# Running the first latent product chunk by chunk, and turning a rarely taken block into loops

## The chip, the cores and the metric

The kernel runs on one core of one Trainium2 chip. The metric is the device time of one execution, in microseconds. Three runs of the kernel before gave 951.0, 952.68 and 953.88 us; their median is 952.68 us. The profile below is of one further execution.

## The reference

The program is a trunk of two layers over 256 tokens of width 1024, batch 1, all in float32. Each layer adds two branches to the residual stream:

```python
mod = silu(c) @ ada_w[l] + ada_b[l]          # shift, scale and gate for both branches
h = rmsnorm(x, norm1_g[l]) * (1 + sc1) + sh1
x = x + g1 * token_mix(h, positions, w_in[l], ...)
h = rmsnorm(x, norm2_g[l]) * (1 + sc2) + sh2
x = x + g2 * grouped_moe(h, w_router, ...)
```

`token_mix` projects `h` once into several sections. One of them is the latent section (384 columns for the queries, 256 for keys and values, 32 for a rotary key) of a multi-head latent attention; the others feed a gated linear recurrence (HGRN2) and the gates. The rotary parts use cos and sin of `positions * inv`. `grouped_moe` picks 2 of 16 experts for each token; every expert has a gate, an up and a down matrix.

## The kernel before

Activations lie transposed, model dimension on the 128 partitions: `xT` is eight blocks (index k) of 128x256. Weights are loaded in float32, in pieces of up to 2 MB, into buffers named A0, A1, B0, B1, C0, C1, x0, x1 and some smaller ones. A weight of the mixer is split into a rounded float32r part and the rest (`split`: a copy on ACT, a subtraction on DVE, L417), so is the activation (`hh`, `hl`), and a product is three matmuls (high x high, low x high, high x low). The split weights live in a ring of four slots (`W`, filled by `wunit`).

The framework traces the program and then orders each engine's instructions by a plan of its own: what is ready goes first, earlier program text before later. Instructions passed to `keep_in_program_order`, the loads through `load` among them, stay behind what was traced before them on their engine. SP issues all DMAs, in one queue.

Layer 0 starts as follows. Before any product, the shift and scale columns of the first norm must be made from `ada_w`: eight quarter matrices of 1 MB, `first[i, q]` with i = 1 for scale and i = 0 for shift and q the quarter of the model dimension. Each quarter is summed over the contraction by eight float32 calls on PE (`ada_rows`, L360), copied out by ACT (`part`, L368), and folded into columns by two small products and a DVE addition (`ada_finish`, L372 to L375). `modulate` (L521 to L528) then makes two blocks of `hh` and `hl` from a normalised block `h` and the columns. The loop at L609 runs the latent product in two halves of the contraction, k = 0..3 with weights `lat` half 0 and k = 4..7 with half 1; within a half the loop over the six output tiles is outside and the four blocks k inside. `first_mod` (L470) runs quarters 0 and 1 before the product begins, and quarters 2 and 3 one sum at a time between the output tiles of the first half. The weights are queued in the order: `vec`, `crow` (the vector c on all partitions), `xT`, positions, four quarters, `lat` half 0 whole, four quarters, `lat` half 1.

`tables` (L425) makes cos and sin of the rotary angles and the lower bounds of the recurrence on DVE and ACT. It stands ahead of the first norm in the program. `masks` follows the latent product. After the latent product come the sections `qf` (four pairs of output tiles), the latents' norms, and the rest of the mixer; while it runs, DVE also works off `ada_steps`, one-megabyte pieces of `ada_w` for the later columns (L384), which use `crow`.

In the mixture of experts each expert has 64 places. `overflow` (L1168) holds a block for tokens beyond them. It is under `tc.If(over > CAP)`, near the end of each layer's mixture, and each engine loads a count and branches over the block (L1172) when no expert is overfull. Inside it lies one loop over expert pairs p, whose body is written out for both experts q and the eight blocks `fb` of the hidden width (`spill`).

Of the kernel before, what the change touches and what calls it, by code (L numbers as in the profile page):

```python
# [19 lines left out]
P = 128  # L20
# [81 lines left out]
def _lay_out(v):  # L102
# [35 lines left out]
    for i, n in enumerate(("w_gate", "w_up", "w_down")):  # L138
# [3 lines left out]
        if i == 2:  # L142
# [5 lines left out]
         "adat": adat, "crow": v["c"], "we": we}  # L148
# [8 lines left out]
def trunk(ctx: ExitStack, tc: tile.TileContext, x, pos, vec_in, msk_in, lat_in, wb, wq_in, wkv_in, ada_in, adat_in, crow_in, we,  # L157
# [47 lines left out]
    nc.sync.dma_start(vec, vec_in)  # L205
# [5 lines left out]
    crow = one.tile([P, D], F32, name="crow")  # L211
    nc.sync.dma_start(crow, bass.AP(tensor=crow_in.tensor, offset=crow_in.offset, ap=[[0, P], [1, D]]))
    xT = one.tile([P, J, T], F32, name="xT")
    nc.sync.dma_start(xT, x)
    posi = solo("vm", [P, T], I32)
    nc.sync.dma_start(posi, bass.AP(tensor=pos.tensor, offset=pos.offset, ap=[[0, P], [1, T]]))
# [5 lines left out]

    def first_load(h):
        for q in (h, h + 1):
            for i in (1, 0):
                nc.sync.dma_start(first[i, h][:, (q - h) * QUART:(q - h + 1) * QUART], ada_in[i, q])

    first_load(0)
# [3 lines left out]
    for l in range(DEPTH):  # L232
        todo.append([("sec", l, n, h) for n in ("lat",) + SECTIONS for h in range(2)])
        todo.append([("moe", l, p, i, h) for p in range(E // 2) for i in range(3) for h in range(2)
                     if (p, i, h) not in ((0, 2, 1), (1, 1, 1))])

    def issue():
        while todo and not todo[0]:
            todo.pop(0)
        for n, part in enumerate(todo[:2]):  # L240
            while part:
# [13 lines left out]
                if key[0] == "sec":  # L255
# [3 lines left out]
                    if key == ("sec", 0, "lat", 0):  # L259
                        first_load(2)  # L260
# [92 lines left out]
    ac.activation(crow, crow, AF.Silu)  # L353
# [10 lines left out]

    def ada_sum(l, s, q, w, part):
        b = bank()
        ada_rows(b[:, :QD], w)
        ac.copy(part, b[:, :QD])  # L368
        return l, s, q, part, v_("four")

    def ada_finish(l, s, q, part, col):
        b = bank()  # L372
        for j in range(2):
            mm(b[:, j:j + 1], part[:, j * P:(j + 1) * P], col, True, True)
        ve.tensor_add(mod[l][:, s, 2 * q:2 * q + 2], b[:, :2], v_("adab", (l * 6 + s) * J + 2 * q, 2))  # L375
# [32 lines left out]
    def normed(b):  # L408
        r = rstd(b)
        hs = []  # L410
        for j in range(0, J, 2):
            hs.append(t2("h"))
            ve.tensor_mul(hs[-1], xT[:, j:j + 2, :], r.unsqueeze(1).to_broadcast([P, 2, T]))
        return hs

# [6 lines left out]
    cosT = one.tile([P, T], F32, name="cosT")  # L422
    sinT = one.tile([P, T], F32, name="sinT")

    def tables():  # L425
# [4 lines left out]
        for o, off, add in ((cosT, 0.25, 1.5707963267948966), (sinT, 0.0, 0.0)):  # L430
# [9 lines left out]
            ac.activation(o, o, AF.Sin)  # L440
        ve.tensor_scalar(sinT, sinT, v_("sgn"), None, op0=ALU.mult)

        lbt = t2("lbt", [P, 4, HEADS])
# [15 lines left out]
    def masks():  # L459
        trif, mskf = t2("trif", [P, P]), solo("vm", [P, len(LEVELS) + 1, P])  # L460
# [5 lines left out]
    tables()  # L466
# [3 lines left out]
    hs0 = normed(b)  # L470

    def first_mod(h, modulate):
        last = None
        for q in (h, h + 1):
            for i in (1, 0):
                part = wk.tile([P, QD], F32, tag="acc", bufs=2, name=nm("part"))
                part = ada_sum(0, i, q, first[i, h][:, (q - h) * QUART:(q - h + 1) * QUART], part)
                if last:
                    ada_finish(*last)
                last = part  # L480
                if (i, q) == (1, h + 1):
                    modulate(2 * h)
                yield
        ada_finish(*last)
        modulate(2 * h + 2)

    def mixer(l, hs, after):
# [33 lines left out]
        def modulate(j):  # L521
            js, h = slice(j, j + 2), hs[j // 2]
# [59 lines left out]
        ready = []  # L582
        if l == 0:
            for _ in first_mod(0, modulate):
                pass
# [30 lines left out]
        if l == 0:  # L616
            masks()
# [734 lines left out]
```

## Time and profile before

| what | value |
|---|---|
| median of three runs | 952.68 us |
| the profiled execution's own time | 950.02 us |
| its span, first to last instruction | 948.2 us |
| PE busy | 893.8 us (94%) |
| DVE busy | 502.1 us (53%) |
| ACT busy | 343.8 us (36%) |
| mean granted TensorE clock | 0.975 |
| read from HBM | 314.58 MB |

PE is TensorE's matmul, PEld its weight load. "Granted clock" is the share of TensorE's full speed. A matmul in float32 leaves two PE rows and two PEld rows for each call, one in float32r one of each. In a row of a timeline the first two numbers are start and duration in us, and the bracket tells how long the engine idled before it and what released it; a name ending in q is the engine's sequencer.

### The profile page before, as it was taken

Reading aid. Unit: us, or ns where it says so; the run is one execution under the profiler, and the core shown is the slowest. Engines: PE = TensorE matmul, PEld = TensorE weight load, DVE = VectorE, ACT = ScalarE, POOL = GpSimd, SP = SyncE. Lnnn points to the kernel's source line nnn. Section 1 sums busy time; section 2 is a strip of 40 time slices with the busy share of each in tenths; the row PEclk is TensorE's granted clock in tenths of the full one; section 3 lists DMA queues with packets and bytes.
Section 4 is the critical chain, followed back from the end, with each engine's and each line's share of the span. In section 5 each row is a group of like instructions: output and inputs, shape, how many; then the busy total and the mean of one; then the engine's idle time right before and its main releaser. Section 6 shows DMA issues by size and latency. Waiting matters only on the chain. (4 is left out here: it accounts for less than half of the span.)

```text
span 948.2 us, 15041 instructions
## 1 busy us (share of the span) xinstructions
PE 893.8 (94%) x6118; PEld 637.0 (67%) x6118; DVE 502.1 (53%) x962; ACT 343.8 (36%) x636; POOL 19.4 (2%) x22
## 2 busy tenths in 40 slices
PE   4899999989989999999879999999998999999985
PEld 3688899989944535353359989999994453535333
DVE  4469899899441323232256968969833132323214
ACT  4465454556341112111146647456542121111103
POOL 0000200000000000000000020000000000000002
PEclk9899999999999999999979999999999999999997
DMA  8995566787799899999977626666779989999981
GB/s 362 429 416 193 222 241 238 317 327 282 308 423 423 346 431 431 431 430 426 419 272 311 276 83 241 276 250 233 294 311 423 425 346 431 431 430 431 427 333 45
DMA packets 35586, 316.75 MB, mean 334 GB/s; under 512 B 3888, under 2 KB 4144, under 8 KB 13744
## 3 DMA queue, kind: packets, MB, share of 16 engines
q1 hardware_dynamic: 35504, 315.64, 81.5%
q8 instruction: 53, 0.87, 0.3%
q14 instruction: 29, 0.24, 0.1%
HBM read 314.58 MB, written 1.05 MB: 333 GB/s over the span
## 5 line engine op out<-in xcount | busy, mean ns | idle before, releaser
L559 PE MATMUL bank<-hA,x 128*128 128x256 f32 x1312 | 241.9, 285 | 5.8 <-ACT x L417 3.8
L559 PEld LDWEIGHTS bank<-hA,x 128*128 128x128 f32 x1312 | 204.5, 191 | 9.3 <-DVE x L417 4.2
L559 PE MATMUL bank<-hB,x 128*128 128x256 f32 x656 | 184.3, 281 | 0.0
L559 PEld LDWEIGHTS bank<-hB,x 128*128 128x128 f32 x656 | 125.6, 191 | 0.2
L1211 DVE TENSOR_TENSOR he<-bank,sg 128x512 f32<-128x512 f32 x16 | 11.1, 692 | 157.0 <-PE bank L1138 157.0
L1237 DVE SCALAR_TENSOR_TENSOR r<-bank,small,r 128x512 fp32r<-128x512 f32 (+1 forms) x36 | 24.7, 690 | 96.5 <-ACT r L1236 96.5
L1236 ACT ACTIVATE r<-bank,small 128x512 fp32r<-128x512 f32 (+1 forms) x36 | 22.8, 639 | 118.3 <-PE bank L1147 118.3
L1165 DVE SCALAR_TENSOR_TENSOR xT<-bank,mod,xT 128x256 f32<-128x256 f32 x128 | 52.6, 476 | 16.0 <-PE bank L182 16.0
L1131 DVE TENSOR_SCALAR o<-bank,acol,mod 128x256 f32<-128x256 f32 x32 | 17.4, 543 | 51.5 <-PE bank L182 45.8
L1147 PE MATMUL bank<-moe_2A,heT 128*64 128x512 f32 (+1 forms) x160 | 33.8, 579 | 11.4 <-PEq L1172 5.4
L1203 ACT ACTIVATE sg<-bank 128x512 f32<-128x512 f32 x16 | 9.6, 597 | 94.8 <-PE bank L1138 94.8
L1138 PE MATMUL bank<-moe_1C,o 128*64 128x512 f32 x192 | 43.3, 593 | 0.0
L1138 PE MATMUL bank<-moe_0B,o 128*64 128x512 f32 x192 | 42.3, 593 | 0.0
L1129 ACT ACTIVATE o<-bank,mod,acol 128x256 f32<-128x256 f32 x32 | 18.1, 564 | 59.4 <-DVE o L1131 52.7
L1224 ACT COPY heT<-bank 128x512 f32<-128x512 f32 x16 | 9.4, 588 | 82.1 <-PE bank L1222 82.1
L1138 PE MATMUL bank<-moe_1A,o 128*64 128x512 f32 x160 | 36.1, 593 | 0.0
L1147 PEld LDWEIGHTS bank<-moe_2A,heT 128*64 128x64 f32 x160 | 13.8, 163 | 27.7 <-issue 25.1
L1138 PEld LDWEIGHTS bank<-moe_0B,o 128*64 128x64 f32 x192 | 13.6, 137 | 26.5 <-issue 25.7
L1138 PEld LDWEIGHTS bank<-moe_1C,o 128*64 128x64 f32 x192 | 13.6, 137 | 26.5 <-issue 26.3
L1147 PE MATMUL bank<-moe_2x,heT 128*64 128x512 f32 (+1 forms) x160 | 29.6, 512 | 0.0
L182 PE MATMUL bank<-C 128*128 128x64 f32 (+1 forms) x240 | 29.2, 272 | 0.0
L1138 PE MATMUL bank<-moe_0x,o 128*64 128x512 f32 x128 | 28.6, 594 | 0.0
(304 smaller groups left out, 1669.3 us busy)
## 6 DMA issues: line engine op xcount, KB each, us to landing
moe_0B<-in_we SPq DMA_DIRECT2D x8, 2048.0 KB, 8.9
moe_1C<-in_we SPq DMA_DIRECT2D x8, 2048.0 KB, 14.6
moe_0x<-in_we SPq DMA_DIRECT2D x8, 2048.0 KB, 15.1
moe_1A<-in_we SPq DMA_DIRECT2D x6, 2048.0 KB, 11.6
moe_2A<-in_we SPq DMA_DIRECT2D x6, 2048.0 KB, 14.1
moe_1x<-in_we SPq DMA_DIRECT2D x6, 2048.0 KB, 18.0
moe_2x<-in_we SPq DMA_DIRECT2D x6, 2048.0 KB, 15.5
moe_2C<-in_we SPq DMA_DIRECT2D x6, 2048.0 KB, 20.1
```

What stands on the lines that cost most here:

```text
L182: return pe.matmul(o, l, r, start=start, stop=stop)
L559: pe.matmul(o, a[:, k, :], b[:, k0 + k, :], start=first and k == 0 and q == 0, stop=last and k == 3 and q == 2)
L1129: ac.activation(o, bq, AF.Identity, bias=sh2[:, j:j + 1], scale=acol[:, j:j + 1])
L1131: ve.tensor_scalar(o, bq, acol[:, j:j + 1], sh2[:, j:j + 1], op0=ALU.mult, op1=ALU.add)
L1138: pe.matmul(b[64 * q:64 * q + 64, :], x(j, q), w[:, o:o + 512], start=(j == 0), stop=(j == J - 1), tile_position=(0, 64 * q))
L1147: pe.matmul(b[64 * q:64 * q + 64].rearrange("p (c n) -> p c n", n=256)[:, c % 2:c % 2 + n], x[:, j, 64 * q:64 * q + 64], _ap(w[:, o:o + 25 ...
L1165: ve.scalar_tensor_tensor(xT[:, j, :], b[:, q * T:(q + 1) * T], g2[:, j:j + 1], xT[:, j, :], op0=ALU.mult, op1=ALU.add)
L1203: ac.activation(sg, bg.rearrange("s (j f) -> s j f", j=FJ), AF.Silu)
L1211: ve.tensor_tensor(he, bu.rearrange("s (j f) -> s j f", j=FJ), sg, ALU.mult)
L1224: ac.copy(heT, b.rearrange("p (j s) -> p j s", j=FJ))
L1236: ac.activation(yv[:, 0, d], b[:, s], AF.Copy, scale=wc)
L1237: ve.scalar_tensor_tensor(yv[:, 1, d], b[:, s], wc, yv[:, 0, d], op0=ALU.mult, op1=ALU.subtract)
```

## The change

1. Loads. `crow` is no longer loaded. `vec`, `xT`, the quarters and the latent weights of layer 0 go through `load` in the order: `vec`, `xT`, then for each chunk c = 0..3 the scale quarter, the shift quarter and the quarter of `lat` that belongs to blocks k = 2c and 2c+1; the positions come after chunk 0.
2. `crow` is made from `ca` (silu of c) by eight float32 products with the identity and two ACT copies.
3. The latent product of layer 0 runs over chunks of the contraction. A chunk splits its weights into two units of four output tiles and one unit (`both`) for tiles 4 and 5 of both blocks; the product of block 2c; in its midst the sums of chunk c+1 (two quarters at a time, one copy of 512 columns, four small products, one addition) and `modulate` for it. All six output tiles accumulate over the whole stage.
4. `modulate` also makes the normalised block h; `first_mod`, `ada_sum`, `ada_finish` and `normed` go.
5. `tables` and `masks` are called after the squares of the latents, cos and sin go through one ACT instruction, and a square root table is asked for at the start.
6. In `overflow` the experts q and the blocks of the hidden width become loops too (three nested loops); the body keeps two halves.

```diff
+    for c in range(4):
+        h, q = c // 2, c % 2
+        for i in (1, 0):
+            load(first[i, 2 * h][:, q * QUART:(q + 1) * QUART], ada_in[i, c])
+        n = slice(q * 2 * N_LAT, (q + 1) * 2 * N_LAT)
+        load(lat0[h][:, n], lat_in[0, h][:, n])
+        if c == 0:
+            load(posi, ...)
...
-    ac.activation(crow, crow, AF.Silu)
+    crow = one.tile([P, D], F32, name="crow")
+    for h in range(2):
+        b = bank()
+        for j in range(4):
+            mm(b[:, j * P:(j + 1) * P], ca[:, 4 * h + j:4 * h + j + 1].to_broadcast([P, P]), ident, True, True)
+        ac.copy(crow[:, h * 512:(h + 1) * 512], b)
...
+    def first_sum(c):
+        b = bank()
+        for i in (1, 0):
+            ada_rows(b[:, i * QD:(i + 1) * QD], first[i, c // 2 * 2][:, c % 2 * QUART:(c % 2 + 1) * QUART])
+        part = wk.tile([P, 2 * QD], F32, tag="acc", bufs=2, name=nm("part"))
+        ac.copy(part, b)
+        return part
+
+    def first_finish(c, part):
+        b = bank()
+        for i in range(4):
+            mm(b[:, i:i + 1], part[:, i * P:(i + 1) * P], v_("four"), True, True)
+        js = slice(2 * c, 2 * c + 2)
+        ve.tensor_add(mod[0][:, 0:2, js], ...)
...
         def modulate(j):
-            js, h = slice(j, j + 2), hs[j // 2]
+            js, h = slice(j, j + 2), t2("h")
+            ve.tensor_mul(h, xT[:, js, :], r0.unsqueeze(1).to_broadcast([P, 2, T]))
...
+        def tiles(n, k, i0, units):
+            for i in range(i0, i0 + 3):
+                wh, wl = (units[n][q][:, i] if i < 4 else units[2][q][:, 2 * (i - 4) + n] for q in range(2))
+                for q, (a, x) in enumerate(((wh, hh), (wl, hh), (wh, hl))):
+                    pe.matmul(bs[i][:, :T], a, x[:, k, :], start=k == q == 0, stop=k == J - 1 and q == 2)
...
         if l == 0:
-            for _ in first_mod(0, modulate):
-                pass
-            second = first_mod(2, modulate)
+            first_finish(0, first_sum(0))
+            modulate(0)
+            for c in range(4):
+                w = take("sec", l, "lat", c // 2)...
+                k = 2 * (c % 2)
+                units = [wunit(w[:, k + n, :4 * P]...) for n in range(2)]
+                units.append(both(w, k))
+                for i in (0, 3):
+                    tiles(0, 2 * c, i, units)
+                part = first_sum(c + 1) if c < 3 else None
+                tiles(1, 2 * c + 1, 0, units)
+                if part is not None:
+                    first_finish(c + 1, part)
+                    modulate(2 * c + 2)
+                tiles(1, 2 * c + 1, 3, units)
...
-        if l == 0:
-            masks()
...
+        if l == 0:
+            tables()
+            masks()
         w = section(l, "qf")
...
-                with tc.For_i(0, E // 2, 1) as p:
-                    for q in range(2):
-                        spill(l, p, q, hT, left[:, :, q::2], g2, room)
+                with tc.For_i(0, E // 2, 1) as p, tc.For_i(0, 2, 1) as q:
+                    spill(l, p, q, hT, left, g2, room)
...
-        for fb in range(F // n):
+        with tc.For_i(0, FJ, 1) as fj:
+            for half in range(2):
```

## Rows read from the trace of the kernel before

**Rows 1.** The page: PE's busy tenths and granted clock in 40 slices of the span.

```profile
PE   4899999989989999999879999999998999999985
...
PEclk9899999999999999999979999999999999999997
```

**Rows 2.** Stretches of the first 200 us: start:end, length, then busy us and instructions of PE, PEld, DVE, ACT and POOL, granted clock, DMA share, GB/s.

```profile
26.00:33.00 7.00, 6.24 (x32) 5.56 (x36) 4.36 (x8) 3.40 (x7) 0.00 (x0) 0.51 1.02 429
33.00:46.00 13.00, 11.83 (x128) 9.09 (x120) 3.47 (x11) 3.63 (x9) 0.00 (x0) 1.00 1.01 427
46.00:50.00 4.00, 3.28 (x13) 3.01 (x14) 3.63 (x7) 2.23 (x5) 0.00 (x0) 0.57 1.01 432
...
80.00:200.00 120.00, 118.40 (x928) 110.67 (x928) 108.44 (x182) 64.94 (x129) 6.97 (x4) 1.00 0.70 263
```

**Rows 3.** The same view of the products at L559 alone (PE and PEld): the latent product, then the first half of `qf`.

```profile
26.70:56.70 30.00, 22.46 (x144) 20.90 (x145) 0.84 1.01 427
56.70:67.60 10.90, 10.90 (x98) 10.88 (x97) 1.00 1.03 429
```

**Rows 4.** Timeline of the start, in order of time: first sums, their copy, the normalised blocks, first `hh`, first latent product.

```profile
15.95 1.93 PE L360 MATMUL bank<-first,ca 128*32 128x256 f32 x32
...
18.28 0.64 ACT L368 COPY part<-bank 128x256 f32<-128x256 f32 x2
18.41 1.75 DVE L405 RECIPROCAL rstd<-rstd 128x256 f32<-128x256 f32 x1 [1.43 <-ACT rstd L404]
...
26.76 0.58 PE L559 MATMUL bank<-hA,x 128*128 128x256 f32 x1 [1.89 <-ACT x L417]
```

**Rows 5.** Issue to landing, in us, of the quarters `first` (eight loads), of both latent halves, and of `ada_0r`'s first load, by the view of a tile; and the first use of `ada_0r`.

```profile
L226 SPq DMA_DIRECT2D first<-in_ada x8: 328/390/548, 2.6 to 12.5; - x8
DMA to landing us min/median/max: 9.9/17.5/20.4
L191 SPq DMA_DIRECT2D sec_lat_0A<-in_lat x1: 679/679/679, 4.8 to 4.8; - x1
DMA to landing us min/median/max: 18.2/18.2/18.2
L191 SPq DMA_DIRECT2D sec_lat_1A<-in_lat x1: 328/328/328, 14.9 to 14.9; - x1
DMA to landing us min/median/max: 21.1/21.1/21.1
L384 DVE CUSTOM_DVE_ANT_0 ada_0r<-ada_0r,crow,vec x2: 1280/1280/1280, 70.8 to 72.0; 128x1024 f32<-128x1024 f32 x2
DMA to landing us min/median/max: 24.3/24.3/24.3
```

**Rows 6.** Timeline of one sum and of the last columns before the second half of the latent product.

```profile
41.42 1.07 PE L360 MATMUL bank<-first,ca 128*32 128x256 f32 x16
...
44.33 0.50 PE L182 MATMUL bank<-vec,part 128*128 128x1 f32 x4
...
46.64 0.69 DVE L528 TENSOR_TENSOR hB<-h,hA 128x512 fp32r<-128x512 f32 x1
46.72 0.58 PE L559 MATMUL bank<-hA,x 128*128 128x256 f32 x1 [1.89 <-ACT x L417]
```

**Rows 7.** DVE alone while it makes the tables (busy us and instructions, clock, DMA share, GB/s), and the first of ACT's table loads then.

```profile
10.00:17.00 7.00, 6.31 (x29) 1.00 1.01 425
...
9.79 1.28 ACT L449 ACT_TABLE_LOAD   x1
```

**Rows 8.** The branches over the overfull block: instructions of L1172 over the whole span (ns min/median/max, first and last start), PE's, ACT's and DVE's; then DVE's own semaphore behind the second branch.

```profile
L1172 PEldq COMPARE_BRANCH  x2: 4892/5480/6068, 469.4 to 916.3; - x2
L1172 ACTq COMPARE_BRANCH  x2: 45/48/50, 470.0 to 917.0; - x2
L1172 DVEq COMPARE_BRANCH  x2: 63/68/72, 471.0 to 918.0; - x2
...
L1172 DVEq EVENT_SEMAPHORE  x1: 21/21/21, 922.0 to 922.0; - x1
```

**Rows 9.** Timeline behind both branches: DVE's last work before, PE's first products after, and the same products later at full clock.

```profile
468.56 3.22 DVE L1165 SCALAR_TENSOR_TENSOR xT<-bank,mod,xT 128x256 f32<-128x256 f32 x8
475.76 5.78 PE L1147 MATMUL bank<-moe_2A,heT 128*64 128x256 f32 x32 [5.40 <-PEq L1172]
484.68 1.95 PE L1147 MATMUL bank<-moe_2x,heT 128*64 128x256 f32 x16
...
915.72 3.22 DVE L1165 SCALAR_TENSOR_TENSOR xT<-bank,mod,xT 128x256 f32<-128x256 f32 x8
922.15 6.16 PE L1147 MATMUL bank<-moe_2A,heT 128*64 128x256 f32 x32 [4.63 <-DVEq L1172]
```

**Rows 10.** Loads of instructions (queue 8: packets, MB, share of the DMA engines) from the start to 469 us and in 472 to 474 us; and stretches as in rows 2: the start to 469 us, and from the last such load before each branch to that branch.

```profile
q8 instruction: 24, 0.39, 0.3%
...
q8 instruction: 1, 0.02, 3.1%
...
0.00:469.00 469.00, 442.10 (x3041) 314.34 (x3042) 255.58 (x498) 170.91 (x315) 8.64 (x13) 0.98 0.87 354
460.00:469.00 9.00, 9.00 (x48) 3.62 (x45) 1.04 (x3) 0.60 (x1) 0.00 (x0) 1.00 1.02 421
909.00:916.00 7.00, 7.00 (x37) 2.80 (x34) 0.89 (x2) 0.00 (x0) 0.00 (x0) 1.00 1.02 422
```

More of the change, by code (lines that the diff above doesn't have):

```diff
@@ L235, in trunk @@
                      if (p, i, h) not in ((0, 2, 1), (1, 1, 1))])
+    for h, t in enumerate(("A0", "A1")):
+        held["sec", 0, "lat", h] = [(0, lat0[h], t)]
+        free.discard(t)
+    del todo[0][:2]
     def issue():
@@ L363, in ada_rows @@
                 tc.keep_in_program_order(op)
[L365 to L375, printed above, removed]
     def ada_steps(sections, wait, gap):
@@ L464, in masks @@
         gp.tensor_copy(msk, mskf)
-    tables()
+    warm(ca[:, 0:1])
     b = bank()
@@ L469, in trunk, with mixer @@
         square_sum(b, q)
[L470 to L487, printed above, removed]
+    r0 = rstd(b)
+    def first_sum(c):
[10 more added lines that the diff above has]
+        js = slice(2 * c, 2 * c + 2)
+        ve.tensor_add(mod[0][:, 0:2, js], b[:, :4].rearrange("p (s j) -> p s j", s=2),
+                      v_("adab").rearrange("p (m s j) -> p m s j", m=DEPTH, s=6)[:, 0, 0:2, js])
+    def mixer(l, r0, after):
         own("C0", "C1", "x0", "x1")
@@ L582, in mixer, with both @@
         ready = []
[L583 to L586 removed]
+        def tiles(n, k, i0, units):
[3 more added lines that the diff above has]
+                    pe.matmul(bs[i][:, :T], a, x[:, k, :], start=k == q == 0, stop=k == J - 1 and q == 2)
+        def both(w, k):
+            u = unit[0] % NW
+            unit[0] += 1
+            v = [W[:, u, i] for i in range(2)]
+            split(*(a[:, 0:2] for a in v), w[:, k:k + 2, 4 * P:5 * P])
+            split(*(a[:, 2:4].rearrange("p k (d n) -> p k d n", d=4) for a in v),
+                  w[:, k:k + 2, k0:k0 + ROPE].unsqueeze(2).to_broadcast([P, 2, 4, ROPE]))
+            return v
+        if l == 0:
+            first_finish(0, first_sum(0))
+            modulate(0)
+            for c in range(4):
+                w = take("sec", l, "lat", c // 2)[:, :4 * N_LAT].rearrange("p (k n) -> p k n", k=4)
+                k = 2 * (c % 2)
+                units = [wunit(w[:, k + n, :4 * P].rearrange("p (i n) -> p i n", i=4)) for n in range(2)]
+                units.append(both(w, k))
[7 more added lines that the diff above has]
+                tiles(1, 2 * c + 1, 3, units)
+                if c % 2:
+                    done("sec", l, "lat", c // 2)
+                if c == 1:
+                    atodo.extend(("ada", *a, q) for a in ada_at[l] for q in range(4))
+                    issue()
         else:
@@ L595, in mixer @@
                 scaled(j, r)
-            second = iter(())
-        for k in (0, 4):
+        for k in (0, 4) if l else ():
             w = take("sec", l, "lat", k // 4)[:, :4 * N_LAT].rearrange("p (k n) -> p k n", k=4)
@@ L608, in mixer @@
                 product(wunit(src), hx, k, bs[i][:, :T], k == 0, k == 4)
-                if k == 0 and i:
-                    next(second, None)
             ready = []
```

83 lines of the change are left out of this document (36 added, 47 removed).

## The prediction

> **What bounds the kernel now.** I read the page first: PE is busy nearly all the time, but three places stand out, the first two slices, the middle and the end, where its busy share and its granted clock fall [rows 1]. Everywhere else PE runs back to back, so time is to be won only where PE idles or runs at half clock. [...] The latent product takes from 26.76 to 56.7 us for 144 matmuls, where the next section needs 10.9 us for 98 [rows 3]. From 80 to 200 us PE is busy 118.4 and DVE 108.4 of 120 us: there both are near their limit, and work newly put on DVE there costs time [rows 2]. The middle and the end are the branches over the overfull block: PE's branch takes 6.07 and 4.89 us, that of ACT and DVE under 0.1 us [rows 8]. PE starts its next products at 475.76 and 922.15 us, DVE's last work before having ended at 471.78 and 918.94 [rows 9].
>
> **The change, part by part.** The sum has a stage term and a branch term.
>
> *Loads.* Between the landings of the two latent halves (23.0 and 36.0 us) lie four quarters and one half, 5.57 MB: 2.33 us per MB [rows 5]. The earliest quarter lands at 2.6 + 9.9 = 12.5 us behind 3.1 MB of loads with its own. Now the second quarter of chunk 0 has 3.5 MB behind it, without `crow`: 12.5 + 0.4 x 2.33 = 13.4 us; the chunk's latent weights 15.0; chunk 1's 21.8; chunk 3's 34.8.
>
> *Start of the product.* Before, 26.76 us. Now: sums of chunk 0 on PE until 14.4 (half of 1.93 us after the last landing [rows 4]), the copy of 512 columns 0.64 (taken from both copies of 256, [rows 4]) to 15.1, small products twice 0.6 to 16.3 (0.50 for two at [rows 6], taken higher). From the end of the small products to the end of `hl` it was 44.83 to 47.33, 2.5 us [rows 6]. So 18.8, say 19.0 us. The norm's reciprocals, which ended at 20.16 [rows 4], wait for `xT` alone and no longer stand behind the tables; I put them at 13.4, before they are needed.
>
> *Length of the product.* 144 matmuls at 10.9/98 = 0.111 are 16.0 us [rows 3]. Six quarter sums at 1.07 are 6.4 [rows 6]. Their small products, 0.6 each, are 3.6. Three times PE waits for `modulate`: 2.5 less the nine products that lie beside it (1.0) is 1.5, together 4.5. The start runs at half clock as before: 32 matmuls in 6.24 us are 0.195 each [rows 2], 0.084 more for 18, 1.5. Sum 32.0, end at 51.0 against 56.7 us: **5.7 us won**. What is late is not the weights (34.8) but this chain through PE, ACT, DVE and back. The weights of `qf` (2.1 MB) follow chunk 3's in the queue and land at 34.8 + 2.1 x 2.33 = 39.7, so `qf` can start at once; the first of the `ada` pieces, which stands pinned on DVE, landed at 59.0 and was used at 70.8 [rows 5], so it has 11.8 us in hand, and 6.1 are left.
>
> *`crow`.* Eight products and two copies at about 6 us, when PE and ACT have nothing else, and 0.5 MB less to load (in the landings above). Cost 0; without that cover, 32 PE rows and twice 0.64 us.
>
> *Tables.* 29 DVE operations, 6.31 us, and table loads of 1.28 us on ACT [rows 7] leave an idle time. Between 33 and 46 us DVE was busy 3.47 of 13 us [rows 2]; they are ready early, so I take 0. The other end: all of it behind the latent product, in the stage where DVE is full: 6.3 us. Late `masks` cost nothing as long as the queue brings them before the recurrence, some 20 us later.
>
> *Other DVE and ACT work* of the stage (four splits for tiles 4 and 5 where there were two) lies in the same gaps: 0, at most one split's 0.7 us for each chunk.
>
> *The overfull block.* It never runs here; what counts is its length in PE's program. Before: 32 float32r products (64 rows) and 2 x (2 + 8 x 24) = 388 float32 products (1,552 rows), 1,616 in all. Now 64 + (2 + 2 x 24) x 4 = 264, plus the control of three loops, which no row shows. PE's instructions come in loads: 24 up to the first branch, for 6,083 rows, 253 each, and one more runs at 472 to 474 us, in the middle of the wait [rows 10]. So the branch waited because its target, 6.4 loads on, was not there. [...]
>
> The new jump is 264/253 = 1.04 loads, up to 1.3 with control. PE loads ahead: the last load ran at 460 us, 93 rows before the branch, and PE had not waited for it. I assume that one load beyond the present one is at hand; then the target is there when the branch's place in its load plus the jump is under 2. The place: 93 rows after the last load for the first branch, 71 for the second, plus some 28 for the time between asking and loading (2.6 us at 93/9 a us) [rows 10], plus 32 for `crow` in front: 0.60 and, the shorter first block counted (1,616 - 264 is 5.3 loads, or 5.1 with control), about 0.3. The sums reach 1.9 and 1.6. Gone waits would give: first branch, 475.76 to 471.78 is 4.0, and 32 products at 2 x 1.95 instead of 5.78 us another 1.9: 5.9. Second: 922.15 to 918.94 is 3.2, and 6.16 to 3.9 another 2.3: 5.5, provided that DVE's hold-up to 922.0 [rows 8] goes with its own shorter block (184 operations to 40). Each of the two is about even, since the next load may also come too late: bounds 0 and 11.4. I take **one of the two, 5.6 us**.
>
> *Sum.* 950.02 - 5.7 - 5.6 = 938.7 for the profiled execution; the median of the runs shown lies 2.66 above it, so 941.4 us.
>
> **The rivals.**
>
> *Both branches come free*: 5.7 + 11.4, 935.6. For it: both places plus jump are under 2. Against: the first has little left. *Neither*: 5.7 alone, 947.0. For it: on PE a single load asked too late costs as much as a far one.
>
> *Each chunk's wait drops the clock.* Waits of 1.89 us stood before both stretches at half clock [rows 2, 4, 6]; mine are 1.5 us, three more of them. In the shorter stretch 13 matmuls took 3.28 us, 1.8 more than at full clock. Three times that eats 5.4 of the 5.7: with one branch, 946.8. [...]
>
> *Nothing*: the tables land behind the latent product (6.3) and no branch is freed: 953.3, no change.
>
> *Slower*: PE stays at half clock through the whole cut stage, since no chunk is long enough to bring it back. Each matmul then costs 0.084 more (126 that I counted at full: 10.6), the sums and small products in the same proportion 7.6: the product ends at 69.2, 12.5 after now, and with one branch the whole is 959.5. It decides once about 60% of the stage's work is at half clock (11.3 of 18.2 us). For it: 10.3 of the present 30 us are at half (26.76 to 33 and 46 to 50); against it: between 33 and 46 us, sums and products mixed, the clock was 1.00 [rows 2].
>
> **Chances.** Forecast 0.33, both 0.20, neither 0.15, clock at each chunk 0.12, nothing 0.08, slower 0.12. A measurement here tells 0.3%, 2.9 us. The two cases near 947 lie 5.7 us off and some of them (0.06) will fall inside it, so faster 0.74, same 0.14, slower 0.12. The range leaves out the slower case and little else: 935 to 953.5; the forecast's own is 938 to 945, its two terms unsure by 2 and 1.5.
>
> **What would show it.** Product's first matmul at 19 us and its end at 51; waits of 1 to 2 us before each chunk's first `hl` product; no half clock after 30 us in the stage; table operations on DVE before 51 us; `ada_0r` used without waiting; PE's branch in one of the two places under 0.2 us and its next product within 1 us of DVE's last work. The forecast is wrong if the product ends after 55 us, if the gain of the stage is gone by 200 us (DVE full), or if both branches behave alike.

## The result, and the profile after

The changed kernel takes **945.14 us** (median of 8 runs, 943.4 to 946.88) where the kernel before, on the same chip, took 953.23: a ratio of 0.9912, 95% interval 0.9885 to 0.9939. The forecast was 941.4 us, range 935 to 953.5. The sign and the range held. The two terms did not: the stage term came out with the other sign, and the branch term was twice its size.

The profiled execution took 944.96 us (span 943.2), close to its median, while the one of before, 950.02, lay under its own. So the two profiles make the change some 3 us worse than the medians do; that is kept in mind wherever an absolute time of one is set against the other.

The page after, PE's busy tenths and granted clock (answers [rows 1]):

```profile
PE   7988999999989999999989999999998999999995
...
PEclk8889999999999999999999999999999999999998
```

In the middle the 8 and 7 of before are 9 and 8, and the clock's 7 is a 9. At the start PE's first slice went from 4 to 7, but its third and fourth fell from 9 to 8, and the clock shows three 8s where it showed one.

The latent product alone (L576, PE and PEld), cut at the starts of its chunks; busy us and instructions, granted clock, DMA share, GB/s (answers [rows 3]):

```profile
17.60:29.00 11.40, 6.81 (x37) 6.13 (x37) 0.75 1.01 423
29.00:39.80 10.80, 6.79 (x36) 5.87 (x36) 0.84 1.01 429
39.80:51.40 11.60, 6.62 (x37) 5.96 (x37) 0.82 1.02 432
51.40:58.50 7.10, 7.10 (x36) 7.04 (x36) 0.57 1.00 423
sum 40.90, PE 27.32 PEld 24.99; mean PE 6.83 PEld 6.25
```

It starts 9 us earlier than before and still ends 1.8 us later. At full clock 36 of these matmuls take 4.0 us [rows 3]; no chunk comes near it. The last one runs without a gap and takes 7.10, the price at half clock (36 at 0.195 [rows 2] are 7.0).

The timeline of PE's first instruction in each chunk, and then of DVE when the product ends (answers [rows 4, 6, 7]):

```profile
17.61 2.72 PE L576 MATMUL bank<-hA,x 128*128 128x256 f32 x11 [1.55 <-ACT hA L514]
...
28.99 1.89 PE L576 MATMUL bank<-hA,x 128*128 128x256 f32 x9 [1.09 <-ACT hA L514]
...
39.84 1.89 PE L576 MATMUL bank<-hA,x 128*128 128x256 f32 x9 [1.08 <-ACT hA L514]
...
51.39 1.93 PE L576 MATMUL bank<-hA,x 128*128 128x256 f32 x7 [2.08 <-ACT x L403]
...
58.51 0.29 DVE L414 CAST ang<-vm 128x256 f32<-128x256 int32 x1
```

Each chunk begins with a wait of 1.1 to 2.1 us, and matmuls of 0.21 us and more instead of 0.11 follow. L414 is the first of the rotation tables: they did not go into DVE's idle time of the first stage, they begin as the product ends. The other part of `tables`, the lower bounds of the recurrence, did go into the stage, and it cost something there. It brought a load of ACT's function table (1.28 us) in front of the last chunk:

```profile
48.22 1.28 ACT L435 ACT_TABLE_LOAD   x1
...
49.74 1.09 ACT L514 ACTIVATE hA<-h,mod,acol 128x256 fp32r<-128x256 f32 x2
```

In the chunk before, the first split of the chunk's weights stood at that place. So the last chunk waits for this split (L403), 2.08 us, where the other two wait 1.09 and 1.08 us for the modulation (L514).

The stretches behind it, all engines (PE, PEld, DVE, ACT, POOL):

```profile
58.50:71.00 12.50, 11.37 (x98) 10.97 (x96) 10.85 (x28) 10.01 (x17) 3.56 (x2) 1.00 0.73 285
71.00:80.00 9.00, 6.92 (x48) 6.21 (x47) 8.00 (x15) 8.74 (x12) 0.00 (x0) 1.00 0.34 142
```

DVE is busy 18.9 of 21.5 us, and PE idles 3.2 us at full clock. The first `ada` piece is used at 80.5 us (70.8 before).

To see where time is lost, the same place of the program is compared, by counting PE's matmuls back from the first branch. The changed kernel passes the 2,600th at 75.5 us, the kernel before at 75.9: up to there nothing is lost or won. The stretches to the 2,400th and on to the 2,000th, before and after, in the columns of all engines:

```profile
75.90:108.00 32.10, 32.10 (x203) 27.83 (x202) 27.85 (x48) 17.27 (x26) 6.97 (x4) 1.00 0.50 184
108.00:155.60 47.60, 47.24 (x403) 45.38 (x402) 45.31 (x74) 27.61 (x65) 0.00 (x0) 1.00 0.69 249
```

```profile
75.50:112.70 37.20, 32.63 (x202) 28.09 (x201) 33.30 (x52) 18.75 (x29) 8.62 (x4) 1.00 0.48 170
112.70:162.80 50.10, 48.02 (x403) 45.97 (x402) 46.58 (x77) 28.02 (x65) 0.00 (x0) 1.00 0.57 212
```

5.1 us go in the first, where DVE has 5.5 us more to do, and 2.5 us in the second.

The branches over the overfull block (L1191, ns; answers [rows 8]):

```profile
L1191 PEldq COMPARE_BRANCH  x2: 318/335/352, 476.9 to 917.2; - x2
```

The timeline behind the first and the second (answers [rows 9]):

```profile
479.50 4.00 PE L1166 MATMUL bank<-moe_2A,heT 128*64 128x256 f32 x32 [1.60 <-DVEq L1191]
...
919.91 3.67 PE L1166 MATMUL bank<-moe_2A,heT 128*64 128x256 f32 x32 [1.60 <-DVEq L1191]
```

6.07 and 4.89 us became 0.35 and 0.32. PE now waits 1.60 us, for DVE's last work before the branch, and the 32 products run at full clock (4.00 and 3.67 us instead of 5.78 and 6.16).

So the balance by these traces is: 7.5 us late at the first branch (476.9 against 469.4), of which some 3 may be the quick execution of before (no row places them); then the branches give them back.

### The profile page after: what moved, and what is told of

Same layout as the page of the kernel before. It is cut to its first block, busy times and chain, and to the rows that moved or that the text cites. A ratio compares the mean times of both kernels' runs of the same rounds, so it can differ in the third digit from the quotient of the medians.

```text
span 943.2 us, 15063 instructions
## 1 busy us (share of the span) xinstructions
PE 896.7 (95%) x6134; PEld 641.3 (68%) x6134; DVE 503.9 (53%) x962; ACT 345.1 (37%) x638; POOL 23.3 (2%) x22
## 5 line engine op out<-in xcount | busy, mean ns | idle before, releaser
L547 PEld LDWEIGHTS bank<-hA,x 128*128 128x128 f32 x1216 | 186.3, 188 | 11.0 <-DVE x L403 7.4
L547 PE MATMUL bank<-hB,x 128*128 128x256 f32 x608 | 169.0, 278 | 0.0
L547 PEld LDWEIGHTS bank<-hB,x 128*128 128x128 f32 x608 | 114.8, 189 | 0.2
L1166 PE MATMUL bank<-moe_2A,heT 128*64 128x512 f32 (+1 forms) x160 | 29.5, 511 | 4.5 <-DVEq L1191 3.2
L576 PE MATMUL bank<-hA,x 128*128 128x256 f32 x96 | 23.8, 360 | 5.9 <-ACT hA L514 3.7
## 6 DMA issues: line engine op xcount, KB each, us to landing
moe_0x<-in_we SPq DMA_DIRECT2D x8, 2048.0 KB, 15.3
moe_2A<-in_we SPq DMA_DIRECT2D x6, 2048.0 KB, 14.4
```

Source lines behind the costliest of these rows:

```text
L547: pe.matmul(o, a[:, k, :], b[:, k0 + k, :], start=first and k == 0 and q == 0, stop=last and k == 3 and q == 2)
L576: pe.matmul(bs[i][:, :T], a, x[:, k, :], start=k == q == 0, stop=k == J - 1 and q == 2)
L1166: pe.matmul(b[64 * q:64 * q + 64].rearrange("p (c n) -> p c n", n=256)[:, c % 2:c % 2 + n], x[:, j, 64 * q:64 * q + 64], _ap(w[:, o:o + 25 ...
```

## The experiments

All ratios are to the kernel before, run on the same chip beside the kernel in question; 0.001 is 0.95 us. An interval reaches about 0.003 to either side, so a difference between two of these kernels of less than some 4 us is not shown by their medians alone.

**The two halves of the change, one at a time.** First the overfull block alone, on the kernel before:

```diff
-                with tc.For_i(0, E // 2, 1) as p:
-                    for q in range(2):
-                        spill(l, p, q, hT, left[:, :, q::2], g2, room)
+                with tc.For_i(0, E // 2, 1) as p, tc.For_i(0, 2, 1) as q:
+                    spill(l, p, q, hT, left, g2, room)
...
-        for fb in range(F // n):
+        with tc.For_i(0, FJ, 1) as fj:
```

> The kernel before with nothing changed but the overfull block, which is written as loops. Theory A (both branch waits go, whatever stands in front of them; in the changed kernel 6.6 us came back at the first branch and 5.9 at the second): 12.5 us less than before, a median near 941, PE's branch under 0.5 us in both places, and the first stage as before (latent product 26.8 to 56.7). Theory B (the branches come free only because the changed first stage, 32 products longer and with its own timing, puts them at another place of their instruction load): one of the two still waits some 5 us, the gain is 5 to 7 us, a median near 947.

Measured: 941.31 us, ratio 0.9873 (0.9841 to 0.9904), 12.2 us less than before.

```profile
L1172 PEldq COMPARE_BRANCH  x2: 352/682/1012, 475.2 to 916.5; - x2
```

PE's branch took 0.35 and 1.01 us. The second is more than the 0.5 us expected, but it lies beside DVE's last work: PE starts its next product 1.58 us after its last one there, as behind the first (1.57). Theory A.

Then the changed kernel with the block of before:

```diff
+                with tc.For_i(0, E // 2, 1) as p:
+                    for q in range(2):
+                        spill(l, p, q, hT, left[:, :, q::2], g2, room)
-                with tc.For_i(0, E // 2, 1) as p, tc.For_i(0, 2, 1) as q:
-                    spill(l, p, q, hT, left, g2, room)
```

> The changed kernel with the overfull block as it was before (unrolled). Theory A (the cut first stage with the later tables costs time, 7.5 us by the first branch, and nothing of it is given back): 7 to 8 us more than before, a median near 960, both branch waits back at 4.9 to 6.1 us. Theory B (the loss in the first stage is only a delay of work that later has slack, and the branches' gain alone is less than it looks): 0 to 3 us more than before.

Measured: 963.39 us, ratio 1.011 (1.008 to 1.014): 9.9 us more than before, so the rest of the change is a loss, and Theory B falls; the loss is somewhat more than Theory A's 7 to 8 us. PE's branch took 6.03 and 4.97 us again. The loss is more than the 3.7 us that the same code costs beside loops (0.9912 less 0.9873, which alone is within the noise). The trace shows where a part of the surplus lies: behind the first branch PE gets through three products and then stands still again, with no releaser, which the kernel before did not.

```profile
483.35 1.08 PE L1166 MATMUL bank<-moe_2A,heT 128*64 128x256 f32 x3 [5.37 <-PEq L1191]
486.55 0.69 PE L1166 MATMUL bank<-moe_2A,heT 128*64 128x256 f32 x2 [2.12 <-issue]
```

From their start the 32 products need 9.2 us there, 5.8 us in the kernel before. One load of instructions (queue 8) runs between 484 and 487 us, where the 2.12 us lie; whether they are its doing was not tested, and the remainder of the surplus stays open.

**The tables.** In the changed kernel, back to their old place:

```diff
     posi = solo("vm", [P, T], I32)
+    load(posi, bass.AP(tensor=pos.tensor, offset=pos.offset, ap=[[0, P], [1, T]]))
...
-    warm(ca[:, 0:1])
+    tables()
     b = bank()
...
         if l == 0:
-            tables()
             masks()
```

> The changed kernel with the rotation tables made at the place that they had before, in front of the squares, with their positions loaded ahead of the first chunk; the masks stay behind the latents' squares. Theory A (of the 7.5 us, the tables behind the latent product cost the part that grows in the qf stage, 3 to 5 us, and the chunks' waits and half clock the rest): 3 to 5 us less than the changed kernel, near 941, the latent product still ending near 58. Theory B (the tables lie beside other work there too, and the loss is all PE's clock): no difference, within 1 us. Theory C (DVE now holds up the first chunk's modulation by its 6.3 us of tables): the product starts some 5 us later and the kernel is not faster than the changed one.

Measured: 940.45 us, ratio 0.9865 (0.9834 to 0.9897), 4.5 us under the changed kernel; the product starts at 18.7 and ends at 52.4. The stretches that follow, in the columns above:

```profile
58.50:71.00 12.50, 12.50 (x96) 12.19 (x94) 6.42 (x12) 7.71 (x12) 1.70 (x2) 0.94 0.95 384
71.00:80.00 9.00, 9.00 (x75) 8.46 (x73) 8.91 (x16) 6.88 (x9) 0.00 (x0) 1.00 0.01 2
```

DVE has 4.4 us less to do in the first of them, PE does not idle, and 171 matmuls run in the 21.5 us where it was 146. But the product had ended 6.1 us earlier, which Theory A did not foresee, so at the same time this kernel is further on in its program; its own wait for a split of `qf`, 2.32 us, lies before 58.5. At the same place of the program, from the 2,600th to the 2,400th matmul before the first branch, it takes 33.0 us and the changed kernel 37.2: some 4 us are the tables'. Theory A in size; behind that place this execution, which took 944.12 us, gives time back at a lower clock (0.94 over the next 400 matmuls), so the two profiles do not show the whole 4.5.

The other way round, e1_loops_only with the tables and masks put late and the product left whole:

```diff
-    tables()
+    warm(ca[:, 0:1])
     b = bank()
...
+        if l == 0:
+            tables()
+            masks()
         w = section(l, "qf")
```

> The kernel before with the overfull block as loops (as in e1_loops_only) and with the rotation tables and the masks behind the latents' squares, as in the changed kernel; the latent product is not cut. Theory A (the late tables are what the changed first stage loses: e1_loops_only and e3_tables_early lie 12.2 and 13.1 us under before, the changed kernel 8.1): a ratio to before some 4 us worse than that of e1_loops_only, near 945, the first qf products held up by DVE's splits behind the tables. Theory B (the loss needs the tables and the cut product together, since it is DVE's work left over from the last chunk that the tables delay): within 1.5 us of e1_loops_only, near 941.

Measured: 948.66 us, ratio 0.9958 (0.9933 to 0.9983). That is 0.0085 over e1_loops_only, 8.1 us, and the two intervals don't touch. Theory A in sign, twice its size: late tables and masks cost without any cutting. In the trace the loss lies behind the product, which ended 1.0 us earlier than in e1_loops_only (55.1 against 56.1): from its end to the 2,000th matmul before the first branch it is 108.3 us against 100.2. How much of that is DVE and how much the lower clock there (0.94 from 109.0 to 163.4 us, 0.83 between 120 and 140) was not separated.

**The chunks.** The sums and the modulation of a chunk written half a chunk earlier, in e3_tables_early and in the changed kernel:

```diff
-                for i in (0, 3):
-                    tiles(0, 2 * c, i, units)
                 part = first_sum(c + 1) if c < 3 else None
-                tiles(1, 2 * c + 1, 0, units)
+                tiles(0, 2 * c, 0, units)
                 if part is not None:
                     first_finish(c + 1, part)
                     modulate(2 * c + 2)
-                tiles(1, 2 * c + 1, 3, units)
+                tiles(0, 2 * c, 3, units)
+                for i in (0, 3):
+                    tiles(1, 2 * c + 1, i, units)
```

> e3_tables_early with each chunk's sums, small products and modulation written one half chunk earlier: the sums of chunk c+1 in front of the first products of chunk c, their small products and modulation behind the first nine, so that 27 products are left to cover them. Theory A (the cut product gains nothing because each chunk waits for its modulation and then runs at half clock): the waits of 1 to 2 us between chunks go, the latent product ends near 50 us and the kernel is 4 to 6 us faster than e3_tables_early, 935 to 937. Theory B (what holds the product is the landing of quarters and latent weights, 2.7 MB for a chunk at 2.33 us per MB, so the sums written earlier only make PE wait for them): it ends no earlier than 55 us and the time is that of e3_tables_early within 2 us.

> The changed kernel with the same reordering as e6_ahead_tables, its tables left behind the latents' squares. Theory A (the two losses of the first stage, the waits between chunks and the late tables, are separate terms): it lies below the changed kernel by as much as e6_ahead_tables lies below e3_tables_early, and above e6_ahead_tables by some 4 us. Theory B (with the product ending earlier the tables fall into a gap of DVE in front of the qf stage): no difference from e6_ahead_tables.

Measured: 943.31 us, ratio 0.9890 (0.9858 to 0.9922) with early tables, no gain over e3_tables_early. The planner's order still left a wait of 1.09 us before two chunks, for the modulation and not for a load, and the product ended at 56.6: Theory B's time without its reason, and Theory A not put to the test. With late tables 942.25, ratio 0.9878 (0.9843 to 0.9912), 3.2 us under the changed kernel, which the intervals don't settle; the 4 us by which Theory A of e7_ahead put it above e6_ahead_tables are not there. In e7_ahead one wait before a chunk was left (2.08 us), the clock over the product rose to 0.90, and it ended at 50.8, the forecast's 51. L576 alone, from the product's start to its end:

```profile
18.40:50.80 32.40, 22.11 (x144) 19.44 (x144) 0.90 1.02 427
```

So the length that I had worked out can be had, with another order, and with fewer waits came more clock (0.90, where the changed kernel had 0.76 from 17.6 to 58.5 us). Against e1_loops_only it brings nothing: its product ends 5.3 us earlier, and 2,000 matmuls before the first branch 0.6 us are left of that (155.7 against 156.3). The same 403 matmuls up to that point, first in e7_ahead, then in e1_loops_only:

```profile
105.70:155.70 50.00, 47.91 (x403) 45.96 (x401) 46.49 (x77) 28.02 (x64) 0.00 (x0) 1.00 0.57 212
```

```profile
108.60:156.30 47.70, 47.49 (x403) 45.69 (x402) 45.35 (x74) 27.63 (x65) 0.00 (x0) 1.00 0.69 248
```

2.3 us go here, at full clock, with DVE nearly as busy as PE in both. The trace of e6_ahead_tables, cut as e7_ahead is but with early tables, parts the two causes, by the 203 matmuls from the 2,600th before the first branch and by these 403:

```profile
74.80:107.90 33.10, 32.08 (x203) 27.52 (x202) 27.82 (x43) 16.96 (x26) 6.85 (x4) 1.00 0.46 162
107.90:158.20 50.30, 47.56 (x402) 45.61 (x401) 47.15 (x80) 27.72 (x65) 0.00 (x0) 1.00 0.60 230
```

The 403 take 50.3 us here too, so the 2.3 us come with the cut product (by what way was not followed further). The 203 take 33.1, against 37.7 in e7_ahead and 37.2 in the changed kernel: some 4 us there are the tables'.

**Is an earlier product worth anything?** e1_loops_only without the first quarter sums:

```diff
-        b = bank()
-        ada_rows(b[:, :QD], w)
-        ac.copy(part, b[:, :QD])
...
-        for j in range(2):
-            mm(b[:, j:j + 1], part[:, j * P:(j + 1) * P], col, True, True)
-        ve.tensor_add(mod[l][:, s, 2 * q:2 * q + 2], b[:, :2], v_("adab", (l * 6 + s) * J + 2 * q, 2))
+        ve.tensor_copy(mod[l][:, s, 2 * q:2 * q + 2], v_("adab", (l * 6 + s) * J + 2 * q, 2))
```

> e1_loops_only without the first eight quarter sums and their small products: the first modulation takes the bias alone (the loads stay), so this leaves out part of the computation and its latent product can start as soon as the latent weights land. No expert goes over its capacity with these values. Theory A (the first stage is on the path: what it ends earlier, the kernel ends earlier): the product ends 7 to 11 us earlier (46 to 50 instead of 57) and the kernel some 8 us under e1_loops_only, near 933. Theory B (the qf and attention stages behind it are held by DVE, by the loads and by the clock, so an earlier product is mostly given back there, as the 4 us by which the reordered product of e7_ahead came earlier were gone by 156 us): at most 3 us under e1_loops_only, 938 to 941, and by 156 us the lead is gone.

Measured: 938.96 us, ratio 0.9839 (0.9812 to 0.9866), only 3.2 us under e1_loops_only, with the product ending at 45.5 instead of 56.1. By the number that would be Theory B. The trace says otherwise: 2,000 matmuls before the first branch the lead is still 6.4 of the 10.6 us (149.9 against 156.3); and the second branch took 4.85 us again, although the block is written as loops. From that branch to PE's last matmul it is 5.2 us more than in e1_loops_only (903.9 to 925.4 against 916.5 to 932.7). Less that it would lie some 8 us below: by this subtraction, which is not a measurement, Theory A holds, and an earlier product is worth most of what it is early.

**The branch.** Jumps of other lengths, everything else as in the kernel before: the blocks of an expert unrolled (e4_q_loop, about 840 rows of PE), or the two experts of a pair unrolled (e8_fj_loop, 464 rows). The cuts are shown against e1_loops_only:

```diff
-        with tc.For_i(0, FJ, 1) as fj:
-            at = bass.ds(fj, 1)
+        for fj in range(FJ):
+            at = slice(fj, fj + 1)
```

```diff
-                with tc.For_i(0, E // 2, 1) as p, tc.For_i(0, 2, 1) as q:
-                    spill(l, p, q, hT, left, g2, room)
+                with tc.For_i(0, E // 2, 1) as p:
+                    for q in range(2):
+                        spill(l, p, q, hT, left[:, :, q::2], g2, room)
```

> The kernel before with a loop over the two experts of a pair, whose sixteen blocks stay unrolled: the jump is some 840 PE rows instead of 1,616 or 264. Theory A (what counts is how many instruction loads of 253 rows the jump skips; 3.3 is too far): PE's branch still takes 4 to 6 us in both places and the time is that of before. Theory B (what counts is something else in the loops, or a jump of some 1,000 rows still finds its target): the branch takes under 0.5 us in both, and the time is that of the kernel with loops alone.

> The kernel before with a loop over the blocks of an expert, the two experts of a pair unrolled: the jump is some 464 PE rows, 1.83 instruction loads of 253. Theory A (one load beyond the present one is at hand, so a jump is free while the branch's place in its load plus the jump stays under 2): 0.6 plus 1.83 and 0.3 plus 1.83 are over 2, so both branches still take 4 to 6 us. Theory B (two loads or more beyond the present one are at hand): both branches under 0.5 us, the time that of loops alone. Theory C (a place in between): the wait is shorter, 1 to 3 us, because the load that is needed is already on its way.

One execution of each was timed: 950.03 and 958.0 us. PE's branch took 5.99 and 5.17 us with the long jump, 5.99 and 5.01 with the short one:

```profile
L1172 PEldq COMPARE_BRANCH  x2: 5012/5500/5988, 474.2 to 922.0; - x2
```

That is the source view of e8_fj_loop; the second wait is the shorter one. Theory A in both: a jump of 464 rows cost as much as one of 1,616 (6.07 and 4.89 us). (A single time of 958 says little more, executions of one kernel lying that far apart: those of before, beside e12_shifted, from 949.3 to 960.62.)

Then the same jump at another place, 24 products of one column ahead of everything else on PE:

```diff
+    b = bank()
+    for j in range(24):
+        mm(b[:, j:j + 1], ident, ca[:, j % J:j % J + 1], True, True)
+    spare = one.tile([P, 24], F32, name="spare")
+    ac.copy(spare, b[:, :24])
```

> e1_loops_only with 24 products of one column more at the very start, where PE has nothing else: 96 more PE rows in front of both branches, no other work changed. In the runs so far a branch was free (0.3 to 1.5 us) where the rows since the last instruction load plus the jump of 264 rows came to 283 to 390, and took 4.9 to 6.1 us from 446 on (e9_no_sums, second branch: 182 rows behind its last load). Theory A (that place decides): the first branch goes from 94 to some 190 rows behind the last load, 454 with the jump, and takes 4 to 6 us again; the second goes from 24 to some 120, 384 with the jump, and stays under 1.5 us; the kernel is some 5 us slower than e1_loops_only, near 947. Theory B (a block written as loops is free wherever the branch stands, and the second branch of e9_no_sums had another reason): both stay under 1.5 us and the time is that of e1_loops_only.

Measured: 951.37 us, ratio 0.9966 (0.9937 to 0.9994), 8.9 us over e1_loops_only. The two branches, and the stretch from the last load of instructions (queue 8) to each of them (PE, PEld, DVE, ACT, POOL):

```profile
L1177 PEldq COMPARE_BRANCH  x2: 328/3232/6137, 473.2 to 920.9; - x2
```

```profile
454.60:473.20 18.60, 18.60 (x93) 6.97 (x90) 2.85 (x5) 1.97 (x3) 0.00 (x0) 1.00 1.02 418
909.30:920.80 11.50, 11.50 (x59) 4.47 (x56) 1.14 (x3) 0.60 (x1) 0.00 (x0) 1.00 1.01 411
```

The first branch now stands 93 + 90 = 183 rows behind its load and takes 6.14 us, the second 115 rows and takes 0.33: Theory A, at both places. The time is worse than the 5 us expected because the 24 products were not free: they stretched from 3.97 to 14.4 us, and the latent product started at 31.7 instead of 27.0.

The same two views for e9_no_sums:

```profile
L1166 PEldq COMPARE_BRANCH  x2: 920/2885/4850, 463.8 to 903.9; - x2
```

```profile
462.30:463.80 1.50, 1.50 (x13) 1.50 (x14) 1.40 (x4) 0.00 (x0) 0.00 (x0) 1.00 1.00 396
885.50:903.90 18.40, 18.40 (x93) 6.87 (x89) 2.72 (x5) 1.91 (x3) 0.00 (x0) 1.00 1.01 422
```

Counted in this way (rows from the last load to the branch, plus the jump without the loops' control, and PE's branch in us):

| kernel, branch | rows + jump | sum | branch |
|---|---|---|---|
| e1_loops_only, 2nd | 23 + 264 | 287 | 1.01 |
| e9_no_sums, 1st | 27 + 264 | 291 | 0.92 |
| changed, 2nd | 47 + 264 | 311 | 0.32 |
| e1_loops_only, 1st | 95 + 264 | 359 | 0.35 |
| e12_shifted, 2nd | 115 + 264 | 379 | 0.33 |
| changed, 1st | 123 + 264 | 387 | 0.35 |
| e10_loops_crow, 1st | 127 + 264 | 391 | 0.35 |
| e9_no_sums, 2nd | 182 + 264 | 446 | 4.85 |
| e12_shifted, 1st | 183 + 264 | 447 | 6.14 |
| e8_fj_loop, 1st, 2nd | 95, 179 + 464 | 559, 643 | 5.99, 5.01 |
| before, 1st, 2nd [rows 10] | 93, 71 + 1,616 | 1,709, 1,687 | 6.07, 4.89 |

Free up to 391, dear from 446; the other kept traces fit (e3_tables_early, e6_ahead_tables and e7_ahead free, 0.32 and 0.35 us each, e5_tables_late at 0.35 and 1.47; e2_stage_only dear at 6.03 and 4.97, e4_q_loop at 5.99 and 5.17). Where the last load had begun only 1.5 us before (e9_no_sums, first) or 1.3 us (e1_loops_only, second), the branch took 0.92 and 1.01 us: in both it ended 2.3 to 2.4 us after the load's beginning.

**What else is in it.** `crow` made on PE and ACT, on e1_loops_only:

```diff
-    nc.sync.dma_start(crow, bass.AP(tensor=crow_in.tensor, offset=crow_in.offset, ap=[[0, P], [1, D]]))
...
+            mm(b[:, j * P:(j + 1) * P], ca[:, 4 * h + j:4 * h + j + 1].to_broadcast([P, P]), ident, True, True)
+        ac.copy(crow[:, h * 512:(h + 1) * 512], b)
```

> e1_loops_only with the row of silu(c) made on PE and ACT from its columns, as in the changed kernel, instead of loaded (0.5 MB less ahead of the first quarters, 1.2 us at 2.33 us per MB). Theory A (the start hangs on the landing of the quarters): first sums, product and end 1 us earlier, 939 to 941. Theory B (it is hidden, or lost again): no difference that can be measured. Theory C (32 more PE rows move the branches past the place in their instruction load from which the target is at hand): one branch waits 5 us again, near 947.

Measured: ratio 0.9854 (0.9827 to 0.9881), 942.51 us beside 956.1 for before. The product started 0.9 us earlier (26.1), and both branches stayed free (0.35 and 0.32 us). Theory A by the start; the total, 1.8 us under e1_loops_only, is too small a step to be told. It is the lowest ratio of the kernels that compute everything, and its interval ends below that of the changed kernel (0.9885): the version to keep, before's first stage with `crow` made on the chip and the block as loops.

And no block at all (the kernel then handles no overfull expert):

```diff
-            with tc.If(over > CAP):
...
+            pass
```

> e1_loops_only with the overfull block left out, branch and all (it never runs with these inputs; the kernel no longer handles an overfull expert). Theory A (as loops the block costs next to nothing, 0.3 to 1.5 us for both branches): 0 to 2 us under e1_loops_only. Theory B (the read of the count and the branch still hold up PE and DVE for some us in each layer): 4 us or more under it.

Measured: ratio 0.9862 (0.9828 to 0.9895), 1.0 us under e1_loops_only: Theory A, nothing more is to be won at the branches.

## Why the prediction was right in time and wrong in its steps

**Branches: the place and the jump decided, as forecast; the term was sized at one instead of two.** The step "I take one of the two, 5.6 us" failed; the rival "Both branches come free" is what happened. e1_loops_only won 12.2 us where the bound was 11.4. The working behind the two prices (4.0 + 1.9 and 3.2 + 2.3) stood: from the first branch to the same product behind it (at 484.6 and 484.7 us) e1_loops_only needs 9.4 us and before 15.3, and from the second branch to the last matmul 16.3 against 21.8: 5.9 and 5.5, as I had. So did the places: 0.60 and about 0.3 of a load were, less the 28 rows added for the time between asking and loading, 125 and some 48 rows; the trace has 123 and 47. That the target was not there is my reading of the load that ran in the middle of the wait [rows 10], and the 2, one load at hand beyond the present one, was my assumption: no run shows either by itself. What the runs show in their place is the sum of rows at which a branch was free (0.32 us at 311, 0.35 at 391) or dear (4.85 us at 446, 6.14 at 447). By the assumption, under 2, both sums (1.9 and 1.6) were free; what failed is the hedge behind it, "each of the two is about even, since the next load may also come too late". A load that had only just begun cost 0.9 and 1.0 us (table), not the whole wait. The runs bracket the boundary: with the same 28 rows it lies between 419 and 474, which is 1.66 to 1.87 loads of 253 without the loops' control, and 1.92 to 2.13 with the 0.26 of a load that I had allowed for it. So the 2 is neither shown nor refuted; what the control counts was not measured.

**Stage: wrong sign.** The forecast was 32.0 us from 19.0 on; it was 40.9 from 17.6 on. Term by term: sums 7.2 (6.4 forecast), small products 3.15 (3.6), PE idle 4.4 (4.5); the records of these lines overlap by 1.1. The matmuls made the difference: 27.3 against 17.5. I had counted three waits of 1.5 us and left the clock alone behind them; that was the rival "Each chunk's wait drops the clock", given 0.12. The trace had it: both waits of 1.89 us of the kernel before stood in front of half clock (0.51 between 26 and 33 us, 0.57 between 46 and 50) [rows 2, 4, 6], and I used that for the rival and not for the sum. Three drops at 1.8 us each would have been 5.4 of the missing 9.8; of the rest, 1.1 is the overlap, and half clock lasted longer than the 13 matmuls that I took the 1.8 from: the last chunk is at 0.57 for all its 36. So the 5.7 us were not won. What was lost beyond that lies behind the product, as the counts of matmuls in the result show: 5.1 us up to the 2,400th before the first branch and 2.5 more up to the 2,000th.

**Tables: a term of 0 that measured 4.5 us in the cut kernel and 8.1 us in the uncut one.** The step "they are ready early, so I take 0" failed: ready is not placed. The code calls them behind the latents' squares, and the planner put the rotation tables there, where DVE is full; my other end, 6.3 us, lies between the two. The lower bounds, which did go into the stage, made its last wait longer.

**Rest.** `crow` at 0 held (e10_loops_crow). The `ada` piece, put at 11.8 us in hand, was used 9.7 us later than before; some 3.5 of that go with the tables (77.1 us with early tables, e3_tables_early; 74.5 with late ones and the product whole, e5_tables_late). All three signs that I named against the forecast occurred: the product ended after 55 us, the stage's gain was gone by 200 us, and both branches behaved alike. That the time came near is luck, one error making up for the other: the branches won some 12 us instead of 5.6, and the rest, where 5.7 were to be won, lost 9.9 us beside the unrolled block (e2_stage_only) and some 4 beside the loops (e1_loops_only against the changed kernel, within the noise).

## What to carry to other kernels

A block that never runs can still cost the jump over it (6.07 and 4.89 us here): count the rows from the last instruction load to the branch plus the rows of the block, and write it as nested loops until the sum stays well under what was found dear (here free up to 391 rows, dear from 446). An edit ahead of it moves the place (96 rows more in e12_shifted, and the first branch went from 0.35 to 6.14 us), so look at the branch again after each. When a product is cut so that PE starts earlier, charge the new waits with the clock behind them (here waits of 1.08 to 2.08 us between chunks, and 0.57 to 0.84 granted in those chunks of the changed kernel, though 1.00 in one of e2_stage_only's), and compare the same matmul far behind the product, not starts. Work that is only "ready early" is no cheaper for it: look up which operations stand in front of it on its engine in program order, since a call moved behind a stage lands behind it.

## What the runs showed that I had not expected

- A jump was either free (0.32 to 0.35 us up to a sum of 391 rows, 0.92 and 1.01 where the last load had just begun, 1.47 once in e5_tables_late, its place not known) or cost the whole 4.85 to 6.14 us (from 446 rows); jumps of 464, 840 and 1,616 rows cost the same: 5.99 and 5.01, 5.99 and 5.17, 6.07 and 4.89 us.
- 96 more rows at the start of PE's program (e12_shifted), or 160 matmuls and their weight loads fewer (e9_no_sums), brought a wait of 6.14 and 4.85 us back in a branch 450 to 900 us later, in code that wasn't touched.
- Executions of one kernel differ by 5 us and more (e1_loops_only: 938.48 to 944.32), and a lower granted clock goes with it in the traces: from the 1,200th to the 800th matmul before the first branch the profiled execution of e1_loops_only needed 66.9 us (256.3 to 323.2), that of before, with the same code there, 63.3 (254.0 to 317.3). Between 270 and 280 us the one ran at 0.74 and the other at 0.91, between 280 and 300 at 0.83 and 1.00 (they are not at the same matmul, so the counts cannot be compared).

```profile
280.00:300.00 20.00, 19.32 (x92) 8.47 (x90) 2.01 (x7) 1.18 (x2) 0.00 (x0) 0.83 1.01 417
```

```profile
280.00:300.00 20.00, 19.32 (x122) 9.68 (x120) 3.21 (x9) 2.92 (x5) 0.00 (x0) 1.00 1.01 414
```

What set off the drop in the one and not in the other was not found.
